# A decoder layer in split single precision: the second MLP matrix taken as Strassen block products, with its running sum in HBM

## The chip, the core and the metric

The kernel runs on one core of a Trainium2 chip. The metric is the device time of one launch in microseconds (us). The kernel before took 1018.76 to 1019.87 us in three runs, median 1019.37 us. The engines are called TensorE (PE in the profile; PEld is its weight load), VectorE (DVE), ScalarE (ACT), GpSimd (POOL) and SyncE (SP, which here only issues DMAs).

## The reference, cut to what matters

One layer for 576 token columns (512 prompt tokens and 64 sample tokens) of width 1024:

```python
h = _rmsnorm(x, g_mix_pre)                 # then three branches, gates, w_out
x = x + _rmsnorm(mixed, g_mix_post)
f = jnp.square(jax.nn.relu(_rmsnorm(x, g_ffn_pre) @ w_ff1)) @ w_ff2
x = x + _rmsnorm(f, g_ffn_post)
x = x + jax.nn.sigmoid(_rmsnorm(x, g_ple) @ w_ple_gate) * (p_l @ w_ple_proj)
```

The change is in the line that computes `f`. `w_ff1` is 1024 x 4096 and `w_ff2` is 4096 x 1024, both float32.

## The kernel before

**Products.** Activations lie feature-major: 128 features on the partitions, 576 columns, worked on as two halves of 288 (`HS`). To reach the accuracy, each float32 operand is split into a high and a low part (`hi`, `lo`: ScalarE rounds to the high part, VectorE subtracts it to get the low part), and each product of two operands is three matmuls: hi x hi, hi x lo, lo x hi. Weights are split the same way: a raw 128 x 1024 panel is loaded by SP into a `wst` (or `xst`) tile, cast on ScalarE to `whi` (L141, L162) and subtracted on VectorE to `wlo` (L142, L163). An ordinary output tile of 128 features is a `unit` (L324): 8 contraction blocks x 3 matmuls x 2 column halves = 48 matmuls of 128 x 288.

**The MLP.** The hidden width 4096 is done in four chunks `c` of 1024. For each chunk, stage f1 computes 8 hidden tiles (first matrix, squared ReLU, split into `fh` and `fl`), and stage f2 multiplies them by the chunk's rows of the second matrix and adds the 8 output tiles into `f` in SBUF (`evac_f`; the first chunk copies on ScalarE, the others add on VectorE, L988). The last four output tiles of chunk 3 are done inside `handover`, which also forms the norm and starts the next matrix.

**Strassen in f1.** In chunks 1 to 3 f1 takes two output tiles at a time as a 2 x 2 block product (Winograd's form of Strassen's scheme): the block rows are the two column halves, the block columns the two output tiles, the inner blocks the two halves of the contraction. Seven products of 4 contraction blocks x 3 matmuls make 84 matmuls where two units make 96. `Pair.prep` (L177 to L200) loads the two raw panels and makes four weight sums t1 to t4 on VectorE (L182, L188, L192, L197, each 128 x 512), then casts and splits four groups: (b11, t3), (t2, b21), (t1, b22) of 1024 columns and t4 of 512. `Operands.make` (L221) makes the four sums of activations (s1, s2, s3, x3); that happens once, in chunk 0, since all f1 stages share one input. `pairs` (L251) sets the order of the seven products of one pair and interleaves the last two of the pair before; `done_a` (L1014) takes the four output blocks out of PSUM: two subtractions (L1025, L1027), four ReLU-and-scale operations (L1029), two squares on ScalarE (L1032, L1033) and two low parts (L1034) for each pair.

**What sets the order.** The program is written in one order, and a scheduling layer places each engine's instructions from it, by the order of issue, by priority (`tc.high_priority`) and by the rotation of the buffers: a tile of a pool with n buffers can be written only when its n-th predecessor has been read for the last time. Each engine then runs its own queue strictly in order. `make` is a generator of weight preparations: each `next(make)` in `pairs` issues one of the four groups, so weights are prepared about one pair ahead. The buffers for it are 3 + 2 tiles of split weights and 2 + 2 raw tiles.

Of the kernel before, what the change touches and what calls it, by code (L numbers as in the profile page):

```python
# [1 line left out]

# [11 lines left out]
P = 128  # L14
# [15 lines left out]
def panels():  # L30

    out = []
# [37 lines left out]
def decoder_step(ctx: ExitStack, tc: tile.TileContext, xT, pT, W, consts, smalls, s0q, s0t, ckT, cv,  # L70
# [49 lines left out]
    plan = panels()  # L120
# [48 lines left out]
    class Pair:  # L169
# [7 lines left out]
        def prep(self, j):  # L177
            Q = 4 * P
            a, c = rawtile(), rawtile()
            load(c, W[j])  # L180
            load(a[:, :4, :], W[j + 1][:, :Q])
            V.tensor_tensor(out=a[:, 4:, :], in0=c[:, :4, :], in1=c[:, 4:, :], op=ALU.add)  # L182
            g = whalves(a)
            self.w["b11"], self.w["t3"] = (g, 0), (g, 4)
            yield
            b = rawtile()
            load(b[:, 4:, :], W[j + 1][:, Q:])
            V.tensor_tensor(out=b[:, :4, :], in0=a[:, :4, :], in1=a[:, 4:, :], op=ALU.add)  # L188
            g = whalves(b)
            self.w["t2"], self.w["b21"] = (g, 0), (g, 4)  # L190
            yield
            V.tensor_tensor(out=c[:, :4, :], in0=c[:, :4, :], in1=a[:, :4, :], op=ALU.add)  # L192
            g = whalves(c)
            self.w["t1"], self.w["b22"] = (g, 0), (g, 4)
            yield
            d = rawtile()
            V.tensor_tensor(out=d[:, :4, :], in0=b[:, :4, :], in1=b[:, 4:, :], op=ALU.add)  # L197
            self.w["t4"] = (whalves(d, 4), 0)
            yield
# [18 lines left out]

    class Operands:


        def __init__(self, xh, xl):
            self.xh, self.xl = xh, xl
            self.s = []

        def make(self, src, j):

            xa, xb = tmpt(), tmpt()
            src(j, xa)
            src(j + 4, xb)  # L230
            t = stmp.tile([P, 4, H], F32, tag="stmp", name=nm("stmp"))
            V.tensor_tensor(out=t[:, 0, :], in0=xb[:, HS[1]], in1=xa[:, HS[1]], op=ALU.subtract)
            V.tensor_tensor(out=t[:, 1, :], in0=xa[:, HS[0]], in1=t[:, 0, :], op=ALU.subtract)
            V.tensor_tensor(out=t[:, 2, :], in0=xa[:, HS[0]], in1=xa[:, HS[1]], op=ALU.add)
            V.tensor_tensor(out=t[:, 3, :], in0=xb[:, HS[0]], in1=t[:, 1, :], op=ALU.subtract)
# [16 lines left out]
    def pairs(js, X, make, done, ahead):  # L252
# [3 lines left out]
        prev = None  # L256
        for i, j in list(enumerate(js)) + [(None, None)]:
            q = None
            if i is not None:
                while len(groups) < i + 1 or "t1" not in groups[i].w:  # L260
                    next(make)
                q = Job()
                q.w, q.n = groups[i].w, i
                q.a, q.e, q.b = bank("pa"), bank("pe"), bank("pbb")
                product(q.a, q.w["b11"], X("a11"), True)
                A.activation(q.b[:, :H], q.a[:, :H], AF.Copy, scale=-1.0)
                product(q.e, q.w["t3"], X("s3"), True)
                q.es = halft()
                A.copy(out=q.es, in_=q.e[:, :H])
                next(make, None)  # L270
            if prev is not None:
                product(prev.e, prev.w["t4"], X("a22"), False)
                done(prev, "c21")
            if q is not None:
                product(q.b, q.w["t2"], X("s2"), False)
                A.copy(out=q.e[:, :H], in_=q.b[:, :H])
                next(make, None)
                product(q.a, q.w["b21"], X("a12"), False)
                done(q, "c11")
            if prev is not None:  # L280
                product(prev.b, prev.w["b22"], X("x3"), False)
                done(prev, "c12")
            if q is not None:
                product(q.b, q.w["t1"], X("s1"), False)
                done(q, "c22")
                next(make, None)
            elif ahead:
                ahead()
            prev = q
# [29 lines left out]
    def mm(w, kw, ps, xh, xl, first, last):  # L319
        hi, lo = w  # L320
        for lhs, rhs, s, e in ((hi, xh, first, False), (hi, xl, False, False), (lo, xh, False, last)):
            for i, p in enumerate(ps):
                if p is not None:
                    PE.matmul(p[:, :H], lhsT=lhs[:, kw, :], rhs=rhs[:, HS[i]], start=s, stop=e)  # L324
# [536 lines left out]
    xhi = ctx.enter_context(tc.tile_pool(name="xhi", bufs=2))  # L861
    xlo = ctx.enter_context(tc.tile_pool(name="xlo", bufs=2))
    xst = ctx.enter_context(tc.tile_pool(name="xst", bufs=2))
    stmp = ctx.enter_context(tc.tile_pool(name="stmp", bufs=1))
    wpools[:] = [(whi, wlo)] * 3 + [(xhi, xlo)] * 2
# [31 lines left out]
    def handover(hin, lin, evac, src, gn, tag, nxt):  # L897
# [49 lines left out]
        if nxt is evac_a:  # L947
            fhl.extend((Act8(F32R, "fh"), Act8(F32R, "fl")))
# [252 lines left out]
```

## Time and profile before

| | |
|---|---|
| median of 3 runs | 1019.37 us (1018.76 to 1019.87) |
| profiled execution | 1018.83 us, of it the span of the trace 1017.1 us |
| granted TensorE clock, mean | 0.998 of full speed |
| PE busy | 1003.0 us, 99% of the span |
| DVE busy | 602.9 us, 59% |
| ACT busy | 383.3 us, 38% |
| POOL busy | 45.5 us, 4% |

The page gives busy time per engine over the whole span. The stages of the MLP lie between 605 and 957 us of the span; chunk 0's f2 starts at 605, and from there f1 and f2 of chunks 1 to 3 follow. An engine's busy share in one stage is read from the table by windows, whose limits were put at the first matmul of each stage.

### The profile page before, as it was taken

What the parts mean: (1) busy time and instruction counts of PE and PEld (TensorE: products, weight loads), DVE (VectorE), ACT (ScalarE), POOL (GpSimd) and SP (SyncE); (2) the same over time, 40 slices, a digit from 0 to 9 for tenths busy, and PEclk for the clock granted to TensorE, in tenths of its full rate; (3) what the DMA queues carried; (4) which work ended last, traced back from release to release, by engine and by line L of the source; (5) the groups of instructions that cost most, each with busy time, mean ns of one, the idle gap of its engine ahead of it and who ended that gap; (6) DMA issues with size and microseconds to landing.
All of it is one profiled execution on the core that took longest, in us unless ns stands there. A gap on an engine that the chain in (4) does not pass through costs nothing.

```text
span 1017.1 us, 17818 instructions
## 1 busy us (share of the span) xinstructions
PE 1003.0 (99%) x7477; PEld 975.5 (96%) x7477; DVE 602.9 (59%) x1125; ACT 383.3 (38%) x656; POOL 45.5 (4%) x52
## 2 busy tenths in 40 slices
PE   9999999999999999999999999999999999999998
PEld 9999999999989988899998999999999999999988
DVE  7433755643535776355528885277448644963986
ACT  7122222222213444323435553256126412653641
POOL 0100112010110000000000100000000000000010
PEclk9999999999999999999999999999999999999999
DMA  7222212222362111235413532124212612551222
GB/s 255 100 81 77 78 53 80 88 95 82 114 215 63 50 62 61 80 104 176 148 42 110 182 92 70 42 84 128 91 42 73 187 43 63 178 208 49 63 80 76
DMA packets 32112, 100.77 MB, mean 99 GB/s; under 512 B 3784, under 2 KB 6888, under 8 KB 31136
## 3 DMA queue, kind: packets, MB, share of 16 engines
q1 hardware_dynamic: 30672, 93.63, 29.0%
q0 software_dynamic: 1216, 5.94, 1.6%
q8 instruction: 58, 0.95, 0.4%
q14 instruction: 22, 0.18, 0.1%
q10 hardware_dynamic: 144, 0.06, 0.0%
HBM read 91.33 MB, written 8.29 MB: 98 GB/s over the span
## 4 chain that ended last, share of the span: by engine, by line
PE 85%; DVE 9%; DMA 2%; ACT 1%; POOL 1%; issue 1%; SPq 0%; POOLq 0%; DVEq 0%; ACTq 0%
PE pm L324 68%; PE pbb L216 5%; PE pa L216 3%; PE pe L216 3%; DVE wlo L142 1%; POOL rs_b L378 1%; DMA wst<-in_W 1%; DVE xl L402 1%; DVE hlf L912 1%; DVE x L913 1%; PE pb L739 1%; PE pb L722 1%; DVE fl L1003 1%; PE pb L747 1%; ACT whi L141 1%
## 5 line engine op out<-in xcount | busy, mean ns | idle before, releaser
L324 PE MATMUL pm<-xh,whi 128*128 128x288 f32 x1120 | 257.8, 302 | 0.4 <-ACT xh L401 0.2
L324 PE MATMUL pm<-xl,whi 128*128 128x288 f32 x1120 | 251.9, 296 | 2.0 <-DVE xl L402 1.9
L324 PE MATMUL pm<-xh,wlo 128*128 128x288 f32 x1120 | 251.4, 296 | 2.1 <-DVE wlo L142 2.1
L141 ACT CAST whi<-wst 128x1024 fp32r<-128x1024 f32 (+1 forms) x130 | 130.9, 1008 | 324.8 <-PE pm L324 252.4
L324 PEld LDWEIGHTS pm<-xh,whi 128*128 128x128 f32 x1120 | 183.8, 189 | 9.9 <-issue 7.1
L324 PEld LDWEIGHTS pm<-xl,whi 128*128 128x128 f32 x1120 | 183.9, 188 | 4.2 <-DVE xl L402 2.9
L324 PEld LDWEIGHTS pm<-xh,wlo 128*128 128x128 f32 x1120 | 183.9, 188 | 2.6 <-DVE wlo L142 2.6
L142 DVE TENSOR_TENSOR wlo<-wst,whi 128x1024 fp32r<-128x1024 f32 (+1 forms) x130 | 152.3, 1173 | 36.8 <-ACT whi L141 33.2
L324 PE MATMUL pm<-fl,whi 128*128 128x288 f32 x512 | 115.5, 297 | 1.9 <-DVE fl L1003 1.9
L324 PE MATMUL pm<-fh,whi 128*128 128x288 f32 x512 | 116.1, 298 | 0.1
L324 PE MATMUL pm<-fh,wlo 128*128 128x288 f32 x512 | 115.5, 297 | 0.0
L410 DVE TENSOR_TENSOR tmp<-pm,rb 128x288 f32<-128x288 f32 x80 | 33.4, 452 | 93.5 <-PE pm L324 93.4
L324 PEld LDWEIGHTS pm<-fl,whi 128*128 128x128 f32 x512 | 84.5, 190 | 2.2 <-DVE fl L1003 2.2
L324 PEld LDWEIGHTS pm<-fh,whi 128*128 128x128 f32 x512 | 84.8, 190 | 0.4 <-ACT fh L1001 0.3
L324 PEld LDWEIGHTS pm<-fh,wlo 128*128 128x128 f32 x512 | 84.5, 190 | 0.0
L162 ACT CAST whi<-wst 128x1024 fp32r<-128x1024 f32 (+1 forms) x48 | 44.6, 942 | 95.2 <-PE pm L324 59.2
L163 DVE TENSOR_TENSOR wlo<-wst,whi 128x1024 fp32r<-128x1024 f32 (+1 forms) x48 | 51.8, 1089 | 27.1 <-ACT whi L162 25.6
L378 POOL TENSOR_TENSOR rs_b<-rs_a,mhalf 128x9 f32<-128x9 f32 (+2 forms) x15 | 33.1, 2209 | 768.5 <-DVE rs_a L377 768.5
L216 PE MATMUL pbb<-xs,whi 128*128 128x288 f32 x288 | 58.2, 295 | 0.0
L988 DVE TENSOR_TENSOR f<-f,pm 128x288 f32<-128x288 f32 x48 | 20.0, 451 | 48.0 <-PE pm L324 48.0
L216 PEld LDWEIGHTS pbb<-xs,whi 128*128 128x128 f32 x288 | 46.2, 188 | 0.0
L216 PE MATMUL pbb<-xs,wlo 128*128 128x288 f32 x144 | 42.5, 295 | 0.0
(249 smaller groups left out, 1468.3 us busy)
## 6 DMA issues: line engine op xcount, KB each, us to landing
wst<-in_W SPq DMA_DIRECT2D x134, 512.0 KB, 3.5
wst<-in_W SPq DMA_DIRECT2D x24, 256.0 KB, 2.6
x<-in_xT SPq DMA_DIRECT2D x10, 288.0 KB, 4.7
dx<-x POOLq DMA_DIRECT2D x2, 1152.0 KB, 4.6
x<-dx SPq DMA_DIRECT2D x2, 1152.0 KB, 7.1
out_yT<-x SPq DMA_DIRECT2D x16, 144.0 KB, 1.8
x<-in_xT SPq DMA_DIRECT2D x3, 576.0 KB, 6.3
tmp<-in_pT SPq DMA_DIRECT2D x4, 288.0 KB, 3.9
```

Of the source, the lines that this page charges most:

```text
L141: A.copy(out=hi[:, c, :], in_=st[:, c, :])
L142: V.tensor_tensor(out=lo[:, c, :], in0=st[:, c, :], in1=hi[:, c, :].bitcast(F32), op=ALU.subtract)
L162: A.copy(out=hi[:, :n, :], in_=raw[:, :n, :])
L163: V.tensor_tensor(out=lo[:, :n, :], in0=raw[:, :n, :], in1=hi[:, :n, :].bitcast(F32), op=ALU.subtract)
L216: PE.matmul(bank[:, :H], lhsT=lhs[:, s + j, :], rhs=rhs, start=start and j == 0 and i == 0, stop=j == 3 and i == 2, skip_group_check=True)
L324: PE.matmul(p[:, :H], lhsT=lhs[:, kw, :], rhs=rhs[:, HS[i]], start=s, stop=e)
L378: G.tensor_tensor(out=b, in0=a, in1=mhalf[:, :nb], op=ALU.pow)
L402: V.scalar_tensor_tensor(lo, src, gain(gi, k), hi.bitcast(F32), op0=ALU.mult, op1=ALU.subtract)
L410: V.tensor_tensor(out=out[:, HS[i]], in0=ps[i][:, :H], in1=r[:, HS[i]], op=ALU.mult)
L722: PE.matmul(p[g][:, i * w:i * w + w], lhsT=aq[grow(g), t + i, 128 * n:128 * n + 128], rhs=ak[grow(g), k0:k0 + w], start=True, stop=True)
L739: PE.matmul(po[grow(g), :], lhsT=avt[:, 128 * chunk + 64 * g:128 * chunk + 64 * g + 64], rhs=sb[g], start=kh == 0, stop=kh == nk - 1)
L988: V.tensor_tensor(out=fm, in0=fm, in1=ps[i][:, :H], op=ALU.add)
```

## The change

The second matrix of chunks 1 and 2 (all 8 output tiles, 4 pairs) and of chunk 3 (4 output tiles, 2 pairs; the other 4 stay ordinary units inside `handover`) becomes block products through the same `pairs`.

* The hidden tiles of a chunk are kept in a `Quads` object (four tiles: column half x half of the contraction), and the four sums of hidden tiles that the second matrix now needs are made by `Operands.make` once for each f1 pair, so 4 times in each of chunks 1 to 3. Each is two groups: one sum with its split (288 columns), three sums with one split of 864 columns.
* The running sum of the second matrix lies in HBM (`df`, 8 tiles of 128 x 576). Chunk 0 copies each output to a `tmp` tile on ScalarE and SP stores it; chunks 1 and 2 bring the four blocks of a pair to two `tmp` tiles (two copies on ScalarE, two subtractions on VectorE) and GpSimd issues one accumulating DMA for each (16 in all, 288 KB each); chunk 3 loads `df` back into `f` and adds on VectorE.
* The squared ReLU works by half: ScalarE squares twice, VectorE subtracts; in chunk 0 a VectorE multiplication (L1002) is thereby dropped. The squares of chunks 1 to 3 and their low parts go from 576 columns to 288.
* The weight sums of a pair use 3 raw tiles and not 4 (t4 is written over the first raw tile), t4's split goes to pool `wpart` of half tiles, and the second pool of split weights has one buffer and not two.
* Weight preparation is one chain over all the pairs of both matrices, and the last two products of a pair are carried over to the next stage (`last`, `rest`). Where a stage of the second matrix begins (`own`), the order of its first pair is b11, b21, t3, t2, t1.

```diff
+        ms = range(8)
+        if c:
+            n = 4 if c < 3 else 2
+            pairs.append((len(out), n, "f2"))
+            ms = [m for j in range(n) for m in (j + n, j)] + list(range(2 * n, 8))
...
+            for i, parts in enumerate((("b11", "t3"), ("t2", "b21"), ("t1", "b22"), ("t4",))):
+                n = 4 * len(parts)
+                if i < 2:
+                    r = rawtile()
+                    raw.append(r)
+                if i == 0:
+                    c = rawtile()
+                    load(c, W[j])
+                    load(r[:, :4, :], b11)
+                    add(r[:, 4:, :], c[:, :4, :], c[:, 4:, :])
...
+                else:
+                    r = raw[0]
+                    add(r[:, :4, :], raw[1][:, :4, :], raw[1][:, 4:, :])
...
+        def make(self, aa, ab):
...
+            V.tensor_tensor(out=t[:, 0, :], in0=aa[0], in1=aa[1], op=ALU.add)
+            split(t[:, :1, :], hi[:, :1, :], lo[:, :1, :])
+            V.tensor_tensor(out=t[:, 1, :], in0=ab[1], in1=aa[1], op=ALU.subtract)
+            V.tensor_tensor(out=t[:, 2, :], in0=aa[0], in1=t[:, 1, :], op=ALU.subtract)
+            V.tensor_tensor(out=t[:, 3, :], in0=ab[0], in1=t[:, 2, :], op=ALU.subtract)
+            split(t[:, 1:, :], hi[:, 1:, :], lo[:, 1:, :])
...
+        if c == 0:
+            t = tmpt()
+            for i in range(2):
+                A.copy(out=t[:, HS[i]], in_=ps[i][:, :H])
+            nc.sync.dma_start(out=df[m], in_=t)
+            return
...
+    def relu2(m, i, t, src, r):
+
+        V.scalar_tensor_tensor(t, src, 0.0, r[:, HS[i]], op0=ALU.max, op1=ALU.mult)
+        if F[0] is None or (i, m // 4) in F[1]:
+            A.activation(t, t, AF.Square)
+            return
+        hi, lo = F[0].at(i, m)
+        A.activation(hi, t, AF.Square)
+        A.activation(t, t, AF.Square)
+        V.tensor_tensor(out=lo, in0=t, in1=hi.bitcast(F32), op=ALU.subtract)
...
+            if which in ("c21", "c12"):
+                G.dma_start(out=df[m], in_=q.t[m2], accum_op=ALU.add)
...
+    for c in range(1, 4):
+        Fc = Quads()
+        F[:] = [Fc, ((1, 0),) if c < 3 else (), Operands(Fc.at)]
+        pairs(4, ops, done_a)
+        n = 4 if c < 3 else 2
+        fops = F[2]
+        if c == 3:
+            rest()
+            f = Act8(F32, "f")
+            for k in (0, 2, 1, 3):
+                nc.sync.dma_start(out=f(k), in_=df[k])
+        pairs(n, fops, done_f(c, n), True)
```

Three places of the built order. First VectorE in the middle of f1 of chunk 2, before: `wst` are raw weights, `fl` the low part of a hidden tile of 576 columns, `pa`, `pe`, `pbb` the PSUM banks of a pair.

```order
L1025 TENSOR_TENSOR tmp1069_8143<-pe1059_8057,hlf1061_8084 128x288
L163 TENSOR_TENSOR wlo1082_8221<-wst1080_8218,whi1081_8220 128x512
L1029 SCALAR_TENSOR_TENSOR tmp1069_8143<-tmp1069_8143,rn2_5405 128x288
L182 TENSOR_TENSOR wst1083_8254<-wst1084_8255 128x512
L188 TENSOR_TENSOR wst1089_8308<-wst1083_8254 128x512
L192 TENSOR_TENSOR wst1084_8255<-wst1084_8255,wst1083_8254 128x512
L1034 TENSOR_TENSOR fl1036_7950<-tmp1069_8143,fh1034_7948 128x576
L1029 SCALAR_TENSOR_TENSOR tmp1087_8275<-pa1076_8188,rn2_5405 128x288
L163 TENSOR_TENSOR wlo1091_8312<-wst1089_8308,whi1090_8311 128x1024
```

The same place after the change, where `fq` are the hidden tiles, `stmp` the four sums of them and `xs` their low parts:

```order
L188 TENSOR_TENSOR wst1129_8440<-wst1130_8441 128x512
L266 TENSOR_TENSOR stmp1127_8430<-tmp1106_8263 128x288
L268 TENSOR_TENSOR stmp1127_8430<-tmp1114_8316,tmp1106_8263 128x288
L188 TENSOR_TENSOR wst1134_8467<-wst1129_8440 128x512
L1056 SCALAR_TENSOR_TENSOR tmp1126_8409<-pa1118_8329,rn2_5414 128x288
L455 TENSOR_TENSOR xs1128_8431<-stmp1127_8430,xs1128_8431 128x288
L269 TENSOR_TENSOR stmp1127_8430<-tmp1106_8263,stmp1127_8430 128x288
L214 TENSOR_TENSOR wlo1132_8446<-wst1129_8440,whi1131_8445 128x1024
L1063 TENSOR_TENSOR fq1088_8130<-tmp1126_8409,fq1088_8130 128x288
L1056 SCALAR_TENSOR_TENSOR tmp1114_8316<-pbb1099_8184,rn2_5414 128x288
L1109 TENSOR_TENSOR tmp1133_8461<-hlf1121_8357,pbb1119_8330 128x288
L214 TENSOR_TENSOR wlo1136_8471<-wst1134_8467,whi1135_8470 128x1024
```

Between the weight operations, which are as before, now stand the operand sums (L266 to L270), their splits (L455) and four low parts of 288 columns in place of two of 576.

TensorE where f2 of chunk 2 begins, before: the last f1 products, then an ordinary unit (`pm`) on the split hidden tiles.

```order
L216 MATMUL pbb1096_8322<-xs872_6467,wlo1093_8317 128x288
L216 MATMUL pbb1096_8322<-xs881_6537,whi1092_8316 128x288 x2
L216 MATMUL pbb1096_8322<-xs881_6537,wlo1093_8317 128x288
L324 MATMUL pm1112_8482<-fh1034_7948,whi1104_8465 128x288
L324 MATMUL pm1113_8483<-fh1034_7948,whi1104_8465 128x288
L324 MATMUL pm1112_8482<-fl1036_7950,whi1104_8465 128x288
```

After the change the first f2 pair stands there: `whi1150`/`wlo1151` are its group (b11, t3), `whi1154`/`wlo1155` its group (t2, b21).

```order
L232 MATMUL pe1161_8689<-xs1147_8576,whi1150_8590 128x288 x2
L232 MATMUL pe1161_8689<-xs1147_8576,wlo1151_8591 128x288
L232 MATMUL pa1158_8660<-fq1107_8281,whi1154_8615 128x288 x2
L232 MATMUL pbb1159_8661<-xs1109_8286,whi1154_8615 128x288
L232 MATMUL pe1161_8689<-xs1157_8651,whi1150_8590 128x288
L232 MATMUL pbb1159_8661<-xs1109_8286,whi1154_8615 128x288
L232 MATMUL pe1161_8689<-xs1157_8651,whi1150_8590 128x288
L232 MATMUL pe1161_8689<-xs1157_8651,wlo1151_8591 128x288
L232 MATMUL pa1158_8660<-fq1107_8281,wlo1155_8616 128x288
```

The unit needed two weight panels made ahead and the hidden tiles; the pair needs its own sums of weights, and the operand sums (`xs1157`, of the last f1 pair). On VectorE `wlo1155` and the low parts of `xs1157` stand at the end of the f1 work:

```order
L214 TENSOR_TENSOR wlo1155_8616<-wst1153_8612,whi1154_8615 128x1024
L455 TENSOR_TENSOR xs1157_8651<-stmp1156_8650,xs1157_8651 128x864
L214 TENSOR_TENSOR wlo1164_8706<-wst1149_8586,whi1163_8705 128x1024
L188 TENSOR_TENSOR wst1148_8585<-wst1153_8612 128x512
L214 TENSOR_TENSOR wlo1166_8724<-wst1148_8585,whi1165_8723 128x512
L1134 TENSOR_TENSOR tmp1171_8748<-hlf1162_8702,pbb1159_8661 128x288
L188 TENSOR_TENSOR wst1167_8727<-wst1168_8728 128x512
```

In the last row stands the first sum of the next pair (t3); its raw panel `wst1168` is loaded by a DMA that waits for the t4 sum three rows above it (`wst1148<-wst1153`), the last reader of the raw tile that the panel takes over.

## Rows read from the trace of the kernel before

**Rows 1.** Page, busy time of the engines: us, share of the span, instructions.

```profile
PE 1003.0 (99%) x7477; PEld 975.5 (96%) x7477; DVE 602.9 (59%) x1125; ACT 383.3 (38%) x656; POOL 45.5 (4%) x52
```

**Rows 2.** Page, chain that ended last: share of the span by engine.

```profile
PE 85%; DVE 9%; DMA 2%; ACT 1%; POOL 1%; issue 1%; SPq 0%; POOLq 0%; DVEq 0%; ACTq 0%
```

**Rows 3.** Windows by stage, chunk 0 f2 on; columns in the first line.

```profile
core 0: us, PE busy (x) PEld busy (x) DVE busy (x) ACT busy (x) POOL busy (x), PEclk, DMA share, GB/s
604.97:660.22 55.25, 53.22 (x386) 52.75 (x386) 26.45 (x36) 19.08 (x32) 0.00 (x0) 0.97 0.19 58
660.22:705.14 44.92, 44.86 (x338) 44.62 (x338) 33.13 (x51) 26.13 (x41) 0.00 (x0) 1.00 0.32 97
705.14:756.32 51.18, 51.18 (x386) 51.18 (x386) 24.52 (x36) 11.93 (x15) 0.00 (x0) 1.00 0.26 81
756.32:801.16 44.84, 44.84 (x339) 44.67 (x338) 34.24 (x53) 25.52 (x39) 0.00 (x0) 1.00 0.33 103
801.16:852.33 51.17, 51.17 (x387) 51.17 (x386) 23.92 (x37) 11.41 (x14) 0.00 (x0) 1.00 0.26 76
852.33:898.93 46.60, 46.25 (x346) 45.66 (x345) 34.90 (x54) 27.86 (x41) 0.00 (x0) 1.00 0.54 186
898.93:937.84 38.91, 38.91 (x294) 38.75 (x293) 19.45 (x33) 18.44 (x35) 0.00 (x0) 1.00 0.28 88
```

**Rows 4.** Windows of 1 us where f2 of chunk 0 begins; columns as before.

```profile
612.00:613.00 1.00, 0.00 (x0) 0.00 (x0) 1.00 (x4) 0.00 (x0) 0.00 (x0) 1.00 0.38 82
613.00:614.00 1.00, 0.87 (x5) 0.87 (x6) 0.90 (x3) 0.03 (x1) 0.00 (x0) 0.82 0.92 360
614.00:615.00 1.00, 1.00 (x6) 1.00 (x5) 0.00 (x0) 1.00 (x1) 0.00 (x0) 0.50 0.29 98
```

**Rows 5.** Timeline of PE there: start, us, instruction, idle before.

```profile
613.13 0.53 PE L324 MATMUL pm<-fl,whi 128*128 128x288 f32 x2 [1.93 <-DVE fl L1003]
```

**Rows 6.** Timeline of DVE before that: start us, us, instruction.

```profile
605.36 0.46 DVE L233 TENSOR_TENSOR stmp<-tmp,stmp 128x288 f32<-128x288 f32 x1
605.73 0.46 DVE L234 TENSOR_TENSOR stmp<-tmp 128x288 f32<-128x288 f32 x1
606.10 0.46 DVE L235 TENSOR_TENSOR stmp<-tmp,stmp 128x288 f32<-128x288 f32 x1
...
609.05 0.81 DVE L1000 SCALAR_TENSOR_TENSOR tmp<-pm,rn 128x288 f32<-128x288 f32 x2
...
611.29 0.75 DVE L1002 TENSOR_TENSOR tmp<-tmp 128x576 f32<-128x576 f32 x1
```

**Rows 7.** Timeline of DVE in f1 of chunk 2.

```profile
770.37 0.68 DVE L192 TENSOR_TENSOR wst<-wst,wst 128x512 f32<-128x512 f32 x1
770.97 0.46 DVE L1029 SCALAR_TENSOR_TENSOR tmp<-tmp,rn 128x288 f32<-128x288 f32 x1
771.34 2.96 DVE L163 TENSOR_TENSOR wlo<-wst,whi 128x1024 fp32r<-128x1024 f32 x3
774.21 0.76 DVE L1034 TENSOR_TENSOR fl<-tmp,fh 128x576 fp32r<-128x576 f32 x1
774.88 0.45 DVE L1029 SCALAR_TENSOR_TENSOR tmp<-pa,rn 128x288 f32<-128x288 f32 x1
```

**Rows 8.** DVE by line and form: busy us, mean ns, idle before.

```profile
L1002 DVE TENSOR_TENSOR tmp<-tmp 128x288 f32<-128x288 f32 x10 | 4.3, 452 | 0.0
```

**Rows 9.** Waits of DVE: us in total, times, longest.

```profile
DVE wlo L163 <- ACT whi L162: 25.6, 17, 5.2
DVE wst L182 <- DMA wst<-in_W: 18.7, 6, 3.6
```

**Rows 10.** Page, DMA issues: count, KB each, median us to landing.

```profile
wst<-in_W SPq DMA_DIRECT2D x134, 512.0 KB, 3.5
...
dx<-x POOLq DMA_DIRECT2D x2, 1152.0 KB, 4.6
```

**Rows 11.** ACT by line and form: the cast of a weight group.

```profile
L162 ACT CAST whi<-wst 128x1024 fp32r<-128x1024 f32 x36 | 37.3, 1050 | 74.0 <-PE pm L324 48.5 <-issue 14.7 <-PE pa L216 3.3
```

More of the change, by code (lines that the diff above doesn't have):

```diff
@@ L1 @@
 from contextlib import ExitStack
+from itertools import chain
 import concourse.bass as bass
@@ L189, in prep @@
[L189 to L199, printed above, removed]
+            b12, b22, b11, b21 = [W[j + q // 2][:, Q * (q % 2):Q * (q % 2) + Q] for q in range(4)]
@@ L250, in decoder_step @@
         pass
[L252 to L270, printed above, removed]
-            if prev is not None:
[L272 to L277, printed above, removed]
+    made = [0]
@@ new lines, in decoder_step, with weights, rest, pairs @@
+    last = []
+    def weights():
+        while len(groups) <= made[0] or "t2" not in groups[made[0]].w:
+            next(make)
+        made[0] += 1
+        return groups[made[0] - 1].w
+    def rest():
+        q = last.pop()
+        product(q.b, q.w["b22"], q.X("x3"), False)
+        q.done(q, "c12")
+        product(q.e, q.w["t4"], q.X("a22"), False)
+        q.done(q, "c21")
+    def pairs(n, X, done, own=False):
+        for i in range(n):
+            if own and i == 0 and last:
+                rest()
+            prev = last.pop() if last else None
+            q = Job()
+            q.w, q.n, q.X, q.done, q.t = weights(), i, X, done, {}
+            q.a, q.b = bank("pa"), bank("pbb")
+            product(q.a, q.w["b11"], X("a11"), True)
+            A.activation(q.b[:, :H], q.a[:, :H], AF.Copy, scale=-1.0)
+            if own and i == 0:
+                product(q.a, q.w["b21"], X("a12"), False)
+                done(q, "c11")
+            q.e = bank("pe")
+            product(q.e, q.w["t3"], X("s3"), True)
+            q.es = halft()
+            A.copy(out=q.es, in_=q.e[:, :H])
+            next(make, None)
+            if prev is not None:
+                product(prev.e, prev.w["t4"], prev.X("a22"), False)
+                prev.done(prev, "c21")
+            product(q.b, q.w["t2"], X("s2"), False)
+            A.copy(out=q.e[:, :H], in_=q.b[:, :H])
+            next(make, None)
+            if not (own and i == 0):
@@ L280, in pairs @@
             if prev is not None:
[L281 to L289, printed above, removed]
+                product(prev.b, prev.w["b22"], prev.X("x3"), False)
+                prev.done(prev, "c12")
+            next(make, None)
+            product(q.b, q.w["t1"], X("s1"), False)
+            done(q, "c22")
+            next(make, None)
+            last.append(q)
     def need(j):
@@ L1076, in decoder_step @@
+    for k in range(4, 8):
+        nc.sync.dma_start(out=f(k), in_=df[k])
+    rest()
+    X1, pps[0] = Act8(F32, "x1"), bigt(F32, "pp")
+    for k in range(2):
+        nc.sync.dma_start(out=X1.t[k], in_=dx[:, 4 * k:4 * k + 4, :])
+    nc.sync.dma_start(out=pps[0], in_=dpp)
+    fhl = F[0].hi, F[0].lo
     XH, XL, rb = handover(*fhl, evac_f, f, 4, "3", evac_y)
```

244 lines of the change are left out of this document (134 added, 110 removed).

## The prediction

> **What bounds the kernel now.** I read the page first: PE is busy for 1003.0 of 1017.1 us and DVE for 602.9 [rows 1], and the chain of waits that ended last runs for 85% over PE and for 9% over DVE [rows 2]. So time comes off where matmuls go, unless DVE takes their place. Whether it does is a question for each stage, so the second view is the table by windows [rows 3]. From f1 of chunk 1 on PE has no idle time to speak of: an f1 stage takes 44.84 to 46.60 us, an f2 stage 51.17. The f2 stage has 384 matmuls by the code, so one matmul is 51.18 / 384 = 133.3 ns; an f1 stage has 4 x 84 = 336, 44.92 / 336 = 133.7 ns. DVE is at 33 to 35 us in an f1 stage (75%) and at 24 in f2 (47%). Only f2 of chunk 0 is off: 55.25 us for the same 384 matmuls, 4.07 more than f2 of chunk 1. There PE stood idle for 1.93 us waiting for the low part of the last hidden tile [rows 5], and after that the granted clock was 0.82 and then 0.50, the level of 1.2 GHz [rows 4]. Of the 4.07 us the idle time is 1.93, which leaves 2.1 us as the price of that clock drop.
>
> **DVE's price list.** What counts in a busy queue is the distance from start to start. For 288 columns it is 0.37 us (605.36, 605.73, 606.10 [rows 6]); for 512 it is 770.97 - 770.37 = 0.60; three splits of 1024, 1024 and 512 take 774.21 - 771.34 = 2.87, so 1.13 for 1024; for 576 it is 774.88 - 774.21 = 0.67 [rows 7]. For the new 864 columns I take 0.97, on the line between 576 and 1024.
>
> **Step 1, matmuls.** A pair of output tiles takes 84 matmuls where two units take 96. Of the second matrix 4 + 4 + 2 = 10 pairs are changed: 120 matmuls fewer, at 133.5 ns: **-16.0 us**. All of it is on PE, thus on the path.
>
> **Step 2, f2 of chunk 0.** The DVE backlog there ends with unit 7 of f1, whose ReLU could only start at 609.05, and the squaring that is dropped stands in that backlog (at 611.29 [rows 6]; three of 576 columns at 0.67 = 2.0 us in the last units, the earlier ten of 288 columns [rows 8] lie in idle time). That is as much as the stall of 1.93. If the stall goes, the clock drop goes with it: between 0 and -4.1, taken **-3 us**.
>
> **Step 3, DVE in the f1 stages.** This is the step that decides. Weight work for a pair, f1 or f2, is four sums (4 x 0.60), three splits of 1024 (3 x 1.13) and one of 512 (0.60): 6.4 us. An f1 pair has beside it 2 subtractions, 4 ReLUs, 3 to 4 low parts, 4 operand sums and a split of 288 columns (14 x 0.37) and one split of 864 (0.97): 6.1 us. So an f1 pair is 12.5 us on DVE against 84 x 0.1335 = 11.2 on PE, where before the same list gave 6.4 + 6 x 0.37 + 2 x 0.67 = 10.0. An f2 pair is 6.4 + 2 x 0.37 = 7.2 against 11.2. Over a chunk DVE needs 79 us of PE's 90, but the buffers hold only about one pair of weights ahead, so f2's slack can't be saved up for the f1 stage that follows.
>
> Walk for chunk 2: DVE's f1 work begins with the first c21 subtraction, 36 matmuls (4.8 us) into the stage. It must have made the low part of the group (t2, b21) of the first f2 pair when PE comes to it, by the order 388 matmuls or 51.8 us into the stage: 47.0 us. In that stretch of its queue stand 15 sums (9.0), 11 splits of 1024 (12.4), 3 of 512 (1.8), 3 of 864 (2.9) and 56 operations of 288 columns (20.7): 46.8 us. That is break-even, so each microsecond in which DVE itself waits is a microsecond of PE. It does wait: the raw panel for t3 of the next pair is loaded only when the t4 sum of this pair has read its tile, 3.5 us of DMA [rows 10], while 2.7 to 2.9 us of other work stand between, so 0.7 us or more at each of three pairs; and each sum goes through a cast on ScalarE (1.05 us [rows 11]) before its split. The trace has both waits at the same places, 18.7 us for the panel and 25.6 for the cast over three f1 stages and more [rows 9]; DVE's idle time in f1 of chunk 2 is 44.84 - 34.24 = 10.6 us [rows 3], much of it spent before full buffers. I take 3 us of waiting, ends 0 and 8. Stall 2.8 us in chunk 2. Chunk 1 begins with nearly two pairs of weights ready, 1.7 us better: 1.1. Chunk 3 has four more low parts (x3's operand tiles are all kept split there), 1.5 us: 4.3. Together **+8.2 us** (0 to 24).
>
> **Step 4, from the first f2 pair to the second.** When that low part is done, DVE still has a split of 864, one of 1024 and the t4 sum (0.97 + 1.13 + 0.60), then the panel (3.5), the t3 sum (0.60), the cast (1.05): 7.9 us. PE has 53 matmuls in hand, 7.1 us, and then waits for the high part 0.8 and for the low part some 0.6: 1.4 us, three times: **+4.2 us** (0 to 6). After that DVE catches up by 4 us for each pair.
>
> **Step 5, clock.** Two of the stalls are longer than the 1.93 us behind which the clock fell; at 2.1 us each I count one: **+2.1** (0 to 6).
>
> **Step 6, the running sum in HBM, at nothing.** The 16 accumulating DMAs wait in POOL's queue, which has no other work there (0.00 busy in all these rows [rows 3]). Each holds a `tmp` tile until it has landed; five tiles at two for each pair of 11.2 us leave some 15 us from issue to reuse. No row shows an accumulating DMA: the nearest are the plain 1152 KB from POOL in 4.6 us and 512 KB from SP in 3.5 [rows 10], a fraction of the size here being 288 KB. So I take about 5 us, hidden; a gain is excluded, since the tile's next writer never waits for less than nothing. If it took over 15 us, the subtraction that writes the next `tmp` tile would wait with the whole DVE queue behind it, and PE for that. The Trainium skill, page "DMA: Bandwidth & Descriptors", section "Anatomy of one DMA - SWDGE (gpsimd) path", gives 2.0 us plus bytes / 436e3 for a plain DMA of this kind; for the 1152 KB row that is 4.7, which agrees, and for 288 KB it is an estimate of 2.7. Chunk 0's stores stand in SP's queue ahead of weight loads that are two units (12.8 us) early; the eight loads of `df` in chunk 3 are needed one f1 pair later: hidden, at most +2 us. ScalarE gets two more copies for a pair and stays under 65%.
>
> **Sum**, against the profiled execution's 1018.83 us: -16.0 - 3.0 + 8.2 + 4.2 + 2.1 = -4.5, so 1014.3 us. That execution lies 0.5 us under the median of the three runs (1019.37), so for the measured time I forecast **1014.8 us**, 0.45% under that median.
>
> **Rivals.**
> (a) DVE's excess is covered. If the casts and panels come while DVE does other work, and it starts the f1 stage with a full pair of weights (6.4 us) made, steps 3 to 5 shrink to some 4 us: 1018.8 - 19 + 4 = **1004**. For it: DVE was 25% idle in f1 without costing PE anything. Against: that idle time was before full buffers, and there is one buffer of split weights fewer.
> (b) Slower: DVE sets the pace of the f1 stages outright. If an operation starts only when the one before it is through, each of the 88 operations of the stretch costs 0.08 to 0.09 us more (0.452 [rows 8] against 0.37), 7.5 us a stage. The stalls of step 3 become 8.2 + 22.5 = 30.7, each long enough for the clock (3 x 2.1): -19 + 30.7 + 4.2 + 6.3 = +22, **1041**; with half of the operations so held, **1029**. It beats the saving from a stall of about 4.5 us a stage on. For it: the operand sums depend on each other (s1 to s2 to x3) and on casts. Against: in the trace operations in a row overlap as soon as they don't need each other [rows 6, 7], and the built order puts other work between. The Trainium skill, page "VectorE: DVE Perf Modes", section "The DRAIN you can't avoid", says that the next operation does not start until the pipe of the one before is empty; by that rule 1041 would be the answer. The rows with 0.37 us from start to start under a duration of 0.46 contradict it here, and the same section allows that an operation that is not held starts earlier.
> (c) The accumulating DMAs take over 15 us, or their landing holds up weight loads: every f2 pair of chunks 1 and 2 then waits, say 3 us for each of 8: **1038**.
> (d) Balance: stalls eat the saving, **1019**: the waits of step 3 at 5 us a stage instead of 3, with one more clock drop.
>
> **How the numbers follow.** Chances: forecast 0.40 (its own range 1009 to 1017), (a) 0.13, (d) 0.14, (b) 0.26, (c) 0.07. Under 0.2% (2 us), a change can't be told from none by runs of this kernel. Faster: the forecast and (a), 0.53; same: most of (d), 0.12; slower: 0.35. The range reaches to (a) and the half-held form of (b), and a little over it: 1004 to 1034; outside lie the worse half of (b), most of (c) and the best of (a).
>
> **What would show it.** In the profile after: PE instructions fewer by 120; the gap before `pm<-fl` at f2 of chunk 0 under 1 us and the clock 1.00 there (step 2); DVE over 95% busy in the f1 stages, with PE gaps of 1 to 5 us released by DVE's L214 where f2 of chunks 1 to 3 begins, the longest in chunk 3 (step 3); a second gap of 1 to 2 us at the second f2 pair, behind a DVE wait for a `wst` panel (step 4); POOL's DMAs landing in under 8 us and no DVE wait on them (step 6). Gaps in the middle of f1 stages, at L455 or L1063, would speak for (b); DVE well under 90% there without a gap for (a); waits of DVE or ScalarE on `df` DMAs for (c).

## The result, and the profile after

The changed kernel took 1031.32 us (median of 4 runs, 1030.95 to 1038.96) against 1019.07 of the kernel before (4 runs): a ratio of 1.0139, 95% interval 1.0116 to 1.0163. It is 1.4% slower; 0.45% faster was forecast. The profiled execution has a span of 1029.2 us where before had 1017.1.

The page of the changed kernel, busy time of the engines and the chain that ended last (they answer to [rows 1, 2]):

```profile
PE 996.8 (97%) x7357; PEld 962.7 (94%) x7357; DVE 665.6 (65%) x1255; ACT 438.7 (43%) x809; POOL 59.3 (6%) x68
...
PE 69%; DVE 20%; DMA 6%; issue 3%; ACT 1%; POOL 1%; DVEq 0%; ACTq 0%; POOLq 0%; SPq 0%
```

PE has 120 instructions fewer, as the change says, but DVE's part of the chain went from 9% to 20% and DMA's from 2% to 6%. Windows of the changed kernel by stage, from f2 of chunk 0 to the last block product of chunk 3; an f1 stage is cut here at the first b11 product of the f2 stage that follows (they answer to [rows 3]):

```profile
core 0: us, PE busy (x) PEld busy (x) DVE busy (x) ACT busy (x) POOL busy (x), PEclk, DMA share, GB/s
604.85:655.88 51.03, 51.03 (x386) 51.03 (x385) 24.09 (x34) 20.44 (x37) 0.00 (x0) 1.00 0.32 110
655.88:698.80 42.92, 42.92 (x327) 42.92 (x325) 37.66 (x68) 28.61 (x56) 0.00 (x0) 1.00 0.26 82
698.80:751.11 52.31, 47.07 (x326) 45.57 (x324) 38.37 (x57) 26.15 (x45) 4.35 (x5) 0.93 0.47 109
751.11:802.39 51.28, 49.05 (x360) 47.98 (x361) 44.51 (x81) 31.05 (x59) 2.55 (x3) 1.00 0.38 100
802.39:854.29 51.90, 45.23 (x316) 43.29 (x314) 35.81 (x53) 24.77 (x42) 4.95 (x6) 0.97 0.47 110
854.29:905.20 50.91, 49.20 (x362) 47.81 (x360) 45.73 (x85) 31.90 (x62) 1.89 (x3) 1.00 0.44 113
905.20:935.33 30.13, 24.90 (x170) 22.91 (x171) 25.52 (x42) 19.26 (x34) 0.00 (x0) 1.00 0.74 270
```

By the built order 648, 672 and 528 matmuls stand between these marks in chunks 1, 2 and 3; at 133.5 ns they need 86.5, 89.7 and 70.5 us. Two rows make a chunk: 95.2, 103.2 and 81.0. So the excess is 8.7, 13.5 and 10.5, together 32.7 us. Against it stand 16.0 for the matmuls and 4.2 in f2 of chunk 0 (51.03 against 55.25): +12.5, which is the change of the span (+12.1) to 0.4.

Who PE waited for (from, to, us in total, times, longest):

```profile
PE pa L232 <- DVE wlo L214: 7.4, 8, 1.6
PE pa L232 <- ACT whi L213: 6.6, 7, 1.6
...
PE pbb L232 <- DVE tmp L1109: 1.8, 2, 1.3
PE pbb L232 <- ACT pe L325: 1.6, 3, 0.5
...
PE pbb L232 <- ACT xs L454: 1.4, 1, 1.4
PE pbb L232 <- DVE xs L455: 1.2, 1, 1.2
```

No wait of the MLP is over 1.7 us, but there are more than twenty of them. Three of them, at the start of f2 of chunk 1, in the timeline of PE, and the granted clock there by windows of 2 us:

```profile
709.02 0.40 PE L232 MATMUL pbb<-xs,whi 128*128 128x288 f32 x1 [1.36 <-ACT xs L454]
710.63 0.61 PE L232 MATMUL pbb<-xs,whi 128*128 128x288 f32 x1 [1.21 <-DVE xs L455]
...
712.00 0.61 PE L232 MATMUL pbb<-xs,whi 128*128 128x288 f32 x1 [0.53 <-ACT pe L325]
```

```profile
708.00:710.00 2.00, 0.40 (x1) 0.19 (x1) 2.00 (x3) 0.97 (x2) 0.00 (x0) 1.00 0.60 195
710.00:712.00 2.00, 0.85 (x2) 0.50 (x2) 1.49 (x3) 0.43 (x2) 0.00 (x0) 0.58 0.83 269
712.00:714.00 2.00, 2.00 (x8) 2.00 (x9) 2.00 (x3) 1.74 (x2) 0.00 (x0) 0.50 0.16 60
```

PE ran only three matmuls between 708 and 712, and within that time, while it waited 1.21 us for the second, its granted clock fell to half (1.00 up to 710.3 us, then 0.50, the level of 1.2 GHz). 0.93 over the 52.31 us of the stage is 3.7 us, and 0.97 in f2 of chunk 2 another 1.6; these are upper bounds, since PE also waited in part of that time.

VectorE's idle spells in f1 of chunk 2, from the first c21 subtraction at 756.91, where the prediction's walk begins, to 802 (every operation that began after a wait of over 0.2 us; the bracket has the wait and what ended it):

```profile
756.91 0.46 DVE L1132 TENSOR_TENSOR tmp<-pe,hlf 128x288 f32<-128x288 f32 x1 [2.16 <-PE pe L232]
758.25 1.42 DVE L188 TENSOR_TENSOR wst<-wst 128x512 f32<-128x512 f32 x2 [0.88 <-DMA wst<-in_W]
760.79 1.23 DVE L214 TENSOR_TENSOR wlo<-wst,whi 128x1024 fp32r<-128x1024 f32 x1 [0.52 <-ACT whi L213]
767.45 0.46 DVE L1063 TENSOR_TENSOR fq<-tmp,fq 128x288 fp32r<-128x288 f32 x1 [0.39 <-ACT tmp L1062]
769.61 1.42 DVE L188 TENSOR_TENSOR wst<-wst 128x512 f32<-128x512 f32 x2 [1.70 <-DMA wst<-in_W]
783.58 0.69 DVE L188 TENSOR_TENSOR wst<-wst 128x512 f32<-128x512 f32 x1 [0.27 <-DMA wst<-in_W]
```

After 769.61 VectorE hardly stops until 809.36, when PE gets the low part that it stood waiting for at f2's first pair. And in f2 of chunk 2 VectorE waits 4 us for a panel, between the t4 sum of one pair (822.79) and the t3 sum of the next (828.85):

```profile
822.79 0.69 DVE L188 TENSOR_TENSOR wst<-wst 128x512 f32<-128x512 f32 x1
824.16 0.69 DVE L214 TENSOR_TENSOR wlo<-wst,whi 128x512 fp32r<-128x512 f32 x1 [0.69 <-ACT whi L213]
828.85 1.42 DVE L188 TENSOR_TENSOR wst<-wst 128x512 f32<-128x512 f32 x2 [3.99 <-DMA wst<-in_W]
```

### The profile page after: what moved, and what is told of

Read it like the earlier page. It is cut to its first block, busy times and chain, and to the rows that moved or that the text cites. A ratio compares the mean times of both kernels' runs of the same rounds, so it can differ in the third digit from the quotient of the medians.

```text
span 1029.2 us, 17964 instructions
## 1 busy us (share of the span) xinstructions
PE 996.8 (97%) x7357; PEld 962.7 (94%) x7357; DVE 665.6 (65%) x1255; ACT 438.7 (43%) x809; POOL 59.3 (6%) x68
## 4 chain that ended last, share of the span: by engine, by line
PE 69%; DVE 20%; DMA 6%; issue 3%; ACT 1%; POOL 1%; DVEq 0%; ACTq 0%; POOLq 0%; SPq 0%
PE pm L373 60%; DMA wst<-in_W 6%; DVE wlo L214 6%; DVE wst L188 4%; DVE tmp L1056 1%; DVE fq L1063 1%; DVE xs L455 1%; PE pbb L232 1%; DVE hlf L962 1%; DVE xl L451 1%; ACT whi L213 1%; PE pb L788 1%; DVE x L963 1%; PE pb L771 1%; PE pa L232 1%
## 5 line engine op out<-in xcount | busy, mean ns | idle before, releaser
L150 ACT CAST whi<-wst 128x1024 fp32r<-128x1024 f32 (+1 forms) x110 | 109.9, 1001 | 279.8 <-PE pm L373 227.5
L151 DVE TENSOR_TENSOR wlo<-wst,whi 128x1024 fp32r<-128x1024 f32 (+1 forms) x110 | 127.6, 1163 | 30.0 <-ACT whi L150 27.3
L232 PE MATMUL pbb<-xs,whi 128*128 128x288 f32 x528 | 110.2, 300 | 6.0 <-DVE tmp L1109 1.8
L214 DVE TENSOR_TENSOR wlo<-wst,whi 128x1024 fp32r<-128x1024 f32 x88 | 94.4, 1088 | 28.2 <-ACT whi L213 28.2
L213 ACT CAST whi<-wst 128x1024 fp32r<-128x1024 f32 x88 | 81.5, 940 | 50.1 <-DVE wst L188 31.6
L459 DVE TENSOR_TENSOR tmp<-pm,rb 128x288 f32<-128x288 f32 x80 | 33.4, 452 | 95.3 <-PE pm L373 95.2
L373 PE MATMUL pm<-fq,whi 128*128 128x288 f32 x384 | 70.3, 296 | 0.0
L188 DVE TENSOR_TENSOR wst<-wst 128x512 f32<-128x512 f32 x66 | 45.5, 689 | 24.0 <-DMA wst<-in_W 23.5
L373 PEld LDWEIGHTS pm<-fq,whi 128*128 128x128 f32 x384 | 58.1, 188 | 0.1
L232 PEld LDWEIGHTS pbb<-xs,wlo 128*128 128x128 f32 x264 | 50.5, 191 | 0.3 <-DVE wlo L214 0.3
L373 PE MATMUL pm<-fq,wlo 128*128 128x288 f32 x192 | 46.1, 294 | 0.0
```

The costliest lines, as they stand in the source:

```text
L150: A.copy(out=hi[:, c, :], in_=st[:, c, :])
L151: V.tensor_tensor(out=lo[:, c, :], in0=st[:, c, :], in1=hi[:, c, :].bitcast(F32), op=ALU.subtract)
L188: V.tensor_tensor(out=out, in0=a, in1=b, op=ALU.add)
L213: A.copy(out=hi, in_=r[:, :n, :])
L214: V.tensor_tensor(out=lo, in0=r[:, :n, :], in1=hi.bitcast(F32), op=ALU.subtract)
L232: PE.matmul(bank[:, :H], lhsT=lhs[:, s + j, :], rhs=rhs, start=start and j == 0 and i == 0, stop=j == 3 and i == 2, skip_group_check=True)
```

## The experiments

The theories were: **O**, the operand sums make VectorE too slow for the f1 stages; **P**, the loop from a t4 sum over the 512 KB panel to the next t3 sum is too long for an f2 pair, so that VectorE never gains a lead there; **D**, the accumulating DMAs slow the panels; and against O, that the latency of the last operand sums counts and not VectorE's load.

**Big panel first.**

```diff
+                if i == 0:
+                    c = rawtile()
+                    load(c, W[j])
                 if i < 2:
                     r = rawtile()
                     raw.append(r)
                 if i == 0:
-                    c = rawtile()
-                    load(c, W[j])
                     load(r[:, :4, :], b11)
```

> The changed kernel with one edit: Pair.prep takes the raw tile of the 512 KB panel (c) before that of the 256 KB half panel (a), so that by the rotation of the raw tiles the big panel gets a tile that was read out a whole pair earlier. Theory P (the loop t4 sum -> 512 KB panel into the tile it frees -> t3 sum -> cast -> split is longer than the 11.2 us that PE has for an f2 pair, so DVE never makes up its lag in the f2 stages and starts the next f1 stage without a lead): the PE gaps of 0.9 to 1.7 us at the second to fourth f2 pairs and at the start of f1 of chunk 2 go, and those where f2 begins shrink; 1014 to 1023 us from 1031, DVE waits for a wst panel fall from 26.9 us to under 10. Theory O (the operand sums of f1 alone make DVE late): 1027 us or more, the gaps where f2 begins stay at 3 to 5 us a stage. Theory D (the accumulating DMAs slow the panels down): 1026 or more, panels still land after 5 us.

Measured: 1026.2 us, ratio to before 1.0069 (1.0042 to 1.0096), some 5 us under the changed kernel. Waits of DVE for a panel went from 26.9 to 12.6 us:

```profile
DVE wst L188 <- DMA wst<-in_W: 12.6, 9, 4.6
```

The PE gaps at the second to fourth f2 pairs and at the start of f1 of chunk 2 are gone: P is real in its place. But those where f2 begins stayed (1.45, 0.78, 0.76 and 0.53 us in chunk 1, with the clock at 0.93 again), and PE has a new gap of 2.52 us at the first ordinary unit. The time lies between the ranges of P alone and of O alone, and at the edge of D's.

**Without operand sums.**

```diff
-            F[2].make(halves(q.t[False]), halves(q.t[True]))
+            F[2].s.append(ops.s[q.n])
```

> The changed kernel without the four operand sums of each f1 pair and their splits in chunks 1 to 3 (the f2 pairs read the sums of x in their place, so the same matmuls run): 2.8 us less of DVE for each f1 pair, 9.7 against PE's 11.2. Theory O: the gaps where f2 begins (3.6, 3.0 and some 4 us, with two clock drops of some 5 us together) all go, 1012 to 1018 us. Theory P: the gaps at the second to fourth f2 pairs (together 3.6 us in chunk 2) and at the first f1 pair of chunk 2 (1.9 us) stay, because they come from the panel loop; 1018 to 1024. Theory D: as P.

Measured: 1009.83 us, 0.9919 (0.9902 to 0.9935): 21 us less, below what O gave. Windows of this kernel, chunks 1 to 3:

```profile
656.06:700.68 44.62, 44.62 (x338) 44.53 (x337) 36.16 (x60) 28.95 (x55) 0.00 (x0) 1.00 0.27 84
700.68:742.71 42.03, 41.95 (x315) 41.50 (x313) 30.05 (x42) 22.31 (x38) 4.34 (x5) 1.00 0.53 124
742.71:793.27 50.56, 48.74 (x363) 47.81 (x362) 41.08 (x68) 28.73 (x55) 2.55 (x3) 1.00 0.43 111
793.27:835.50 42.23, 42.10 (x315) 41.41 (x313) 29.53 (x42) 21.58 (x38) 4.28 (x5) 1.00 0.49 122
835.50:890.00 54.50, 50.64 (x361) 49.48 (x362) 42.04 (x71) 30.10 (x59) 2.56 (x3) 0.97 0.68 213
890.00:914.50 24.50, 23.50 (x171) 22.58 (x170) 18.73 (x32) 15.70 (x30) 0.00 (x0) 1.00 0.38 110
```

Chunk 1's excess fell from 8.7 to 0.2 us and chunk 2's from 13.5 to 3.1; the gaps at the later f2 pairs went too, which P alone did not expect. Chunk 3 kept 8.5 of its 10.5, with a clock drop in it, so most of its excess does not come from its own sums; with the big panel first as well (below) it is 4.7, and what causes the rest stays open. The edit also takes the casts of the sums off ScalarE, so by itself it does not tell VectorE's load from ScalarE's; the kernel with the scale deferred, below, does.

**Without the accumulating DMAs.**

```diff
-            if which in ("c21", "c12"):
-                G.dma_start(out=df[m], in_=q.t[m2], accum_op=ALU.add)
```

> The changed kernel without the 16 accumulating DMAs of chunks 1 and 2 (the running sum then lacks these two chunks); all else as it is. Theory D: the 512 KB panels in f2 land after 3.5 us as elsewhere, not after 4.9 to 5.3, the gaps at the second to fourth f2 pair fall under 0.5 us: 1022 to 1026. Theory P: the loop gets 1 to 1.5 us shorter where an accumulating DMA ran beside the panel, some of these gaps shrink, 1026 to 1030. Theory O: no change, 1030 to 1032.

Measured: 1028.26 us, 1.0096 (1.0073 to 1.0119), 3 us less. The wait shown above as 3.99 us is 2.30 here, and DVE's panel waits are 20.9 us in place of 26.9:

```profile
824.67 1.42 DVE L188 TENSOR_TENSOR wst<-wst 128x512 f32<-128x512 f32 x2 [2.30 <-DMA wst<-in_W]
```

D exists and is small.

**Operand sums on GpSimd** (with the big panel first).

```diff
-            V.tensor_tensor(out=t[:, 0, :], in0=aa[0], in1=aa[1], op=ALU.add)
+            G.tensor_tensor(out=t[:, 0, :], in0=aa[0], in1=aa[1], op=ALU.add)
```

(and so for the other three sums)

> c_first and besides all operand sums (four of 288 columns for each group, those of x too) on GpSimd and not on VectorE. DVE gets 1.5 us back for each f1 pair (12.5 to 11.0 us). With P and O both at work: under c_first by 3 to 8 us and under the kernel before (1019), 1008 to 1016. If only P is at work: as c_first within 2 us. If GpSimd takes over 1 us for a sum, or its sums slow VectorE's operations at the shared memory port, splits come late: PE gaps released by xs L455 and a time above c_first.

Measured: 1044.62 us, 1.0263 (1.0241 to 1.0285), 18 us above the big panel alone. A sum takes GpSimd about 1 us, and VectorE's low part of a hidden tile, which reads two tiles of SBUF, went from 454 to 612 ns. Groups by line and form of this kernel, GpSimd's third sum, and VectorE's low parts of weights and of hidden tiles; then the low part of a hidden tile with the big panel first:

```profile
L270 POOL TENSOR_TENSOR stmp<-tmp,stmp 128x288 f32<-128x288 f32 x16 | 18.5, 1158 | 1.3
```

```profile
L215 DVE TENSOR_TENSOR wlo<-wst,whi 128x1024 fp32r<-128x1024 f32 x66 | 86.9, 1316 | 39.4 <-ACT whi L214 39.1
...
L1064 DVE TENSOR_TENSOR fq<-tmp,fq 128x288 fp32r<-128x288 f32 x56 | 33.4, 612 | 1.5 <-ACT tmp L1063 1.5
```

```profile
L1064 DVE TENSOR_TENSOR fq<-tmp,fq 128x288 fp32r<-128x288 f32 x56 | 24.8, 454 | 2.8 <-ACT tmp L1063 2.8
```

The mean of 612 ns hides two sorts: the 37 low parts that overlapped no sum of GpSimd's took 451 ns (441 to 460), the 19 that overlapped one took 925 on average and up to 1082. Timeline of the two engines where one of them fell beside two sums:

```profile
882.95 1.08 DVE L1064 TENSOR_TENSOR fq<-tmp,fq 128x288 fp32r<-128x288 f32 x1
...
882.91 0.81 POOL L267 TENSOR_TENSOR stmp<-tmp 128x288 f32<-128x288 f32 x1 [8.48 <-ACT tmp L1063]
883.69 1.02 POOL L269 TENSOR_TENSOR stmp<-tmp,tmp 128x288 f32<-128x288 f32 x1
```

The Trainium skill, page "SBUF - State Buffer", section "Who interferes with whom", says that a VectorE instruction with two inputs in SBUF contends with a GpSimd instruction that reads SBUF. These rows agree. PE waited at `wlo` (9.3 us in 4 waits), at ScalarE's copy of a bank (8.6 in 5) and at VectorE's subtractions (7.7 in 3), and not at `xs`, where the expectation put the gaps; how the 18 us divide between GpSimd's slower sums and VectorE's slower operations is not shown.

**Big panel first, without operand sums.** The two edits above in one kernel.

> c_first and no_opsums in one kernel (big panel first, and the operand sums of chunks 1 to 3 left out as in no_opsums). If the panel loop and the operand sums each cost their own time, the two gains (5 and 21 us) add up: 1003 to 1006 us. If the panel loop costs only where DVE is late from the sums anyway, nothing is added to no_opsums: 1008 to 1011. PE without any gap would be at some 1000 us (before, less 16.0 for the matmuls, less 4 for f2 of chunk 0).

Measured: 1007.17 us, 0.9881 (0.9863 to 0.9899), 2.7 us under the kernel without sums alone: between the two expectations. With the sums out, the panel loop seems to cost less than the 5 us above, but the intervals, some 1.8 us each way, do not tell 2.7 from 5.

**Chunk 3's f2 as units** (with the big panel first).

```diff
-            n = 4 if c < 3 else 2
-            pairs.append((len(out), n, "f2"))
+            n = 4
+            if c < 3:
+                pairs.append((len(out), n, "f2"))
...
-        pairs(n, fops, done_f(c, n), True)
+        if c < 3:
+            pairs(4, F[2], done_f(c, 4), True)
```

> c_first with f2 of chunk 3 as ordinary units again, so that chunk 3 needs no operand sums of hidden tiles; chunks 1 and 2 stay as in c_first. 24 matmuls more (+3.2 us). Theory O at the size that no_opsums showed (about 7 us a chunk): the stalls of chunk 3 (79.7 us for 528 matmuls, 9 us over 70.5, and 3 us behind it) go, 1026 - 12 + 3 = 1015 to 1019. If chunk 3's stalls come from its loads of df (share of the DMA engines 0.74 there) and not from the sums: they stay with df's loads, 1024 to 1029.

Measured: 1020.12 us, 1.0016 (1.0005 to 1.0027), 6 us less in spite of 24 more matmuls, and a little above the expected 1015 to 1019. This is nearer to O than to the rival that chunk 3's stalls come from the loads of `df`, which this kernel keeps. With VectorE as loaded as it is, the two pairs of chunk 3 cost more than they save.

**ReLU on ScalarE, scale deferred** (with the big panel first). The scale r of a token column, which is above zero, passes through ReLU and square as r squared and through the second matrix unchanged; it is put into the norm behind it.

```diff
-        V.scalar_tensor_tensor(t, src, 0.0, r[:, HS[i]], op0=ALU.max, op1=ALU.mult)
+        A.activation(t, src, AF.Relu)
...
+    def stats_f(sq_sum, rb, i):
+        rn, r4 = kept
+        V.tensor_tensor(out=sq_sum[:, HS[i]], in0=sq_sum[:, HS[i]], in1=r4[:, HS[i]], op=ALU.mult)
+        stats(sq_sum, rb, i)
+        V.tensor_tensor(out=rb[:, HS[i]], in0=rb[:, HS[i]], in1=rn[:, HS[i]], op=ALU.mult)
```

> c_first, and the row scale r of the norm before the MLP is taken out of the squared ReLU (it goes as r squared through the second matrix and is put into the norm behind it, four short VectorE operations in all), so that the ReLU of a block is one operation on ScalarE and not one on VectorE: 4 x 0.37 = 1.5 us less of DVE for each f1 pair (12.5 to 11.0 against PE's 11.2), 1.6 us more of ScalarE. Theory O by DVE's throughput: half of what no_opsums gained (2.8 us a pair gave 21), so 10 to 12 us under c_first: 1013 to 1017. If instead the latency of the last operand sums at the boundary decides (sum, cast, split after the last f1 block), the stall at each f2 start stays: 1022 to 1027.

Measured: 1010.04 us, 0.992 (0.9906 to 0.9935): faster than both kernels, 16 us under the big panel alone and a little under O's range. Windows of this kernel, chunks 1 to 3:

```profile
654.43:699.10 44.67, 44.67 (x339) 44.58 (x338) 39.05 (x64) 36.38 (x74) 0.00 (x0) 1.00 0.27 84
699.10:741.83 42.73, 42.03 (x314) 41.50 (x313) 32.22 (x47) 23.93 (x43) 4.34 (x5) 1.00 0.55 128
741.83:793.10 51.27, 49.35 (x363) 48.43 (x361) 43.79 (x72) 36.47 (x75) 2.55 (x3) 0.99 0.41 105
793.10:836.20 43.10, 43.01 (x314) 42.50 (x313) 31.89 (x46) 23.98 (x42) 4.28 (x5) 0.98 0.54 127
836.20:886.85 50.65, 48.53 (x362) 47.83 (x361) 42.96 (x73) 36.41 (x78) 2.57 (x3) 1.00 0.42 107
886.85:911.50 24.65, 23.40 (x171) 22.61 (x170) 21.23 (x38) 17.26 (x33) 0.00 (x0) 1.00 0.83 304
```

The excess is 0.9, 4.7 and 4.8 us. The operand sums, with their casts and splits, are all still there, at the end of f1 as before: what went is 1.5 us of VectorE for each f1 pair. So VectorE's load decides, and not the latency of the last sums by itself. Nor is it ScalarE's load: the edit adds to that, and PE gains. Of the 16.7 us between the two spans (1025.2 and 1008.5), 13.2 lie between the first and the last block product; the rest lies before and behind, where the ReLU and the norm were changed as well.

**Both.** Scale deferred and chunk 3's f2 as units.

> defer and c3_units in one kernel. By theory O both gains add up: 1004 to 1010, under the kernel before (1018). By the latency theory: 1013 to 1017, since then only chunk 3's part goes.

Measured: 1009.11 us, 0.9908 (0.9893 to 0.9923), the same as the one before within the interval. The gains don't add: with the ReLU off VectorE, chunk 3's pairs cost what they save.

**Scale deferred, raw tiles as in the changed kernel.**

> The changed kernel with the row scale taken out of the squared ReLU as in defer, but the raw tiles in the changed kernel's own order (half panel a first, so the 512 KB panel waits for the t4 sum again). Does the panel loop of the f2 stages cost on its own, or only when VectorE is late from f1? On its own (loop 11.7 us against PE's 11.2 in an f2 pair, so gaps of 0.5 to 1.5 us at the second to fourth f2 pairs and no lead for the next f1): 1015 to 1020 us, 5 or more over defer (1010). Only with a late VectorE: 1009 to 1012.

Measured: 1014.91 us, 0.9966 (0.9956 to 0.9976): 5 us over the kernel with the big panel first, just under the range in which the loop costs on its own. Where it costs is less clear: in its profiled execution (1012.71 us, the fastest of nine) PE waited for split weights not at the second to fourth f2 pairs of chunks 1 and 2, as expected, but at the first two f1 pairs of chunk 3 (0.35, 0.33 and 0.70 us) and in f2 of chunk 3 (1.23). Its longest wait, 1.85 us in the fourth f2 pair of chunk 1, was for a copy that stood behind a weight cast in ScalarE's queue. So four kernels make a table: 1031.3 as changed, 1026.2 with the panel first, 1014.9 with the scale deferred, 1010.0 with both. By these medians each edit is worth the same with and without the other, 5 us and 16; the intervals of the four are 1 to 3 us each way.

## Why the prediction was wrong

The mechanism was named (VectorE near break-even in the f1 stages, short waits where f2 begins, one rival that ended slower), but the stalls were taken at 14.5 us with the clock and came to 32.7. Steps 3 and 4 failed, in their sizes. The trace gives the 32.7 by place when one counts from the start of each matmul to the start of the next, less 133.5 ns: 17.4 us are waits in the f1 stages and in the first f2 pair of a chunk (4.8, 6.0 and 6.6 in chunks 1 to 3; step 3 said 8.2), 8.8 are waits at later f2 pairs and at the first f1 pair of chunk 2 (step 4 said 4.2), 4.1 are matmuls at half clock (step 5 said 2.1), and 2.3 are spread over some 1800 matmuls.

* **Step 1** (-16.0) was right: 7357 against 7477 matmuls, and where PE had no wait they ran at the old spacing.
* **Step 2** (-3) was right: the wait of [rows 5] is gone, 51.03 us at clock 1.00 against 55.25, so all 4.2.
* **Step 3** (+8.2) is the term that was mis-sized. Its parts held: the 864-column split took 1057 ns and the next operation began 0.97 us after its start, and VectorE's own waiting in f1 of chunk 2 sums to 3.8 us (0.88, 0.52, 0.39, 1.70, 0.27) where 3 was taken. But a walk at break-even passes each small miss on in full: VectorE began a microsecond later than counted, waited 0.8 longer and took nearly two more for the operations listed (13 of them were followed by one that began only as they ended, some 0.08 us later than listed), and was ready at 809.36 where the walk allowed 802.9 and forecast 2.8 us more. PE paid for it in part inside the f1 stage, where no wait was forecast: 1.64 us at 787.90, in the last pair. The walk also followed one item only, the low part of (t2, b21). In chunk 1 PE waited for another, the cast and split of the last operand sums (1.36 and 1.21 us), which was not in it. VectorE was busy for 88, 87 and 90% of the f1 stages, where over 95% was named as the sign. All that the f1 sums cost, with the clock drops they bring, is 21 us by the kernel without them.
* **Step 4** (+4.2) named the right loop and ended it too early. "After that DVE catches up by 4 us for each pair" is the sentence that failed. The panel of each next pair waits for the t4 sum of the one before, so the loop repeats at every f2 pair, and VectorE enters the next f1 stage with no lead. PE met it at the second, third and fourth pair of chunk 2 (4.2 us), at the second of chunk 3 (2.3) and at the first f1 pair of chunk 2 (2.3); in chunk 1 the later pairs had no gap. Putting the big panel first removed these gaps and was worth 5 us.
* **Step 5** (+2.1) took one drop behind one long stall of over 1.93 us. No wait was that long. Both drops of the MLP came in the second of two shorter waits (1.36 and 1.21 us; 1.50 and 0.97), and cost 4.1 us by the count above. Similar gaps in f2 of chunk 3 left the clock at 1.00; why is open.
* **Step 6** (nothing) was nearly right: the accumulating DMAs landed in 4.5 us where 5 was taken, and no engine waited for a `tmp` tile; but DVE waits 6 us less for panels without them, and they are worth 3 us.
* **Rivals.** (b) had the outcome, not its mechanism: most of VectorE's operations still overlapped (0.37 us from start to start in the f1 stages), only 13 of the 88 were so held, 1.1 us and not 7.5, and the rule quoted there from the Trainium skill, taken alone, does not describe these rows. That its half-held form, 1029, lies near the measured 1031.3 is luck, and so is it that the time lies in the stated range of 1004 to 1034, which was carried up to that form. (c)'s mechanism was there at an eighth of the price it was given (3 us against 24). (d) was summed wrongly: 2 us more of waiting in three stages and one more clock drop give 1022, not 1019.

The gaps that the trace itself counts sum to only 21.1 us, because the count starts at the modelled end of the matmul before, 0.30 us after its start, while matmuls follow each other at 0.13; from start to start nothing of the 32.7 is left over. What stays open is what keeps chunk 3 at 8.5 us without its sums.

## What to carry to other kernels

When a change moves work from the bound engine to one that is 75% busy, count that engine's work for the stage against the stage's new, shorter time: at break-even every wait on it, however well hidden before, becomes the bound engine's. Look for the lead that hides it (buffers of prepared weights) and walk it through the cheap stages too: a buffer that is freed by the last step of one round and filled by a slow DMA for the first step of the next makes a loop of fixed length, which slack on the engine does not shorten. And the order in which tiles are taken from a rotating pool is a free knob: the biggest transfer should get the tile that was freed first (here worth some 3 to 5 us).

## What the runs showed of the hardware

GpSimd takes 0.96 to 1.16 us on average for a 128x288 float32 sum for which VectorE takes 0.45. A VectorE subtraction of two SBUF tiles of that size took 925 ns on average where it overlapped such a sum, and 451 where it did not. An accumulating DMA of 288 KB into HBM landed after 4.5 us (median of 16), a plain store of that size from SP after 2.1. Without the 16 accumulating DMAs, VectorE's waits for weight panels fell from 26.9 to 20.9 us.
